# Tokens of an attention tile ordered column by column instead of row by row, in a hybrid convolution and neighbourhood-attention block on Trainium2

## The chip, the cores and the metric

The kernel runs on one core of one Trainium2 chip. The metric is the device time of one execution in microseconds (us); lower is better. A core has five engines that run their own instruction queues: TensorE (PE, matmuls and transposes), VectorE (DVE), ScalarE (ACT), GpSimd (POOL) and SyncE (SP, which here only issues DMAs). Sixteen DMA engines move data between the chip's memory (DRAM here) and the on-chip memory, whose 128 partitions are the rows of every tile. A line such as L411 is line 411 of the kernel before.

## The reference

One layer of a bidirectional encoder block on 1024 tokens of 1024 channels, in float32. The tokens form a grid of 16 rows by 64 columns (token = 64 * row + column).

```python
def reference(x, ...):
    h = rms_norm(x, norm1_g)
    a, gate, q, k, v = split(h @ w_in)              # 512 columns each
    conv_out = silu(layer_norm(dwconv31(a * sigmoid(gate)) + dw_bias))   # along the 1024 tokens
    q, k = rms_norm per head of 64 (8 heads)
    attn_out = neighbourhood_attention(q, k, v, rpb)
    x = x + concat([conv_out, attn_out]) @ w_out
    h = rms_norm(x, norm2_g)
    return x + (silu(h @ w_gate) * (h @ w_up)) @ w_down                  # 2816 hidden columns
```

In the attention, every query sees a window of 8 grid rows by 16 grid columns, clamped inside the grid, and a learned bias `rpb` by the offset of row and column is added to the scores before the softmax.

## The kernel before

**Tokens and tiles.** Up to the attention, a tile of 128 tokens is two whole grid rows (`t` of 0 to 7 in `nat`, `head_sq`, `head_T`). From the queries on, a tile is a rectangle of 8 grid rows by 16 grid columns: tile `4 * rh + cb` holds the rows `8 * rh` to `8 * rh + 7` and the columns `16 * cb` to `16 * cb + 15`. All 128 queries of such a tile share one window of 12 rows by 24 or 32 columns of keys (`WIN`). The order of the 128 tokens inside the rectangle is free, as long as every place agrees that lays tokens out or reads them. In the kernel before they stand row by row: position `16 * i + j` for row `i` and column `j`.

**Where the order appears.** Five places know it.

- `head_T` (L403 to L413) transposes the normalised queries of two grid rows on TensorE into a PSUM tile `zt` and copies them with two ScalarE activations (L411, one for each grid row) into `qT`, in the order of the rectangles.
- `table` (L592 to L603) loads the bias tables. `tf[rh, ty]` lies in DRAM as [8 rows, 16 columns, 8 heads, 12 * window columns]; a table in on-chip memory has one partition for each query of the rectangle, so the DMA (L601) reads 128 rows in the order of the queries. There are three kinds of column block (`ty`) and two row halves (`rh`).
- `conv_silu` (L777 to L783) transposes the normalised convolution output, which is in the natural order of tokens, applies SiLU on ScalarE, and splits the result into a rounded part `hi` (ScalarE, L107) and a remainder `lo` (VectorE, L111). Both are written into `cm` in the order of the rectangles, so that each tile of the output projection reads 128 adjacent columns.
- `rows` (L785 to L787) gives the DRAM view of the 128 tokens of a rectangle. `load_x2` (L789) uses it to load the residual `x`, and
- `store` (L1221) uses it for the output, half of the channels at a time.

Everything between these places (scores, softmax, output projection, second norm, feed-forward block) works on tiles of 128 tokens and needs no order.

**Order of the work.** The program is scheduled by hand. `nat` and `glu_step` run the input projections as three matmuls for each block (`mac`, L113 to L117, since each operand is held as `hi` and `lo`), with small jobs (`woven`, taken by `weave`) between the blocks; the queries' transposes are such a job, seven blocks into the next projection. Before them, ScalarE takes the squares of the next tile (`head_sq`), VectorE scales it (`head_scale`, `zn`). The depthwise convolution runs beside this on VectorE, with a few taps on ScalarE and GpSimd.

The attention goes over eight rectangles in the order `order` (L617), four steps `i` each, with two heads to a step: `score_mm` (L629), `score_max` (L641, which adds the table), `score_exp` (L646), `score_norm` (L657, GpSimd), `flip` (L665, transposes), `weigh` (L681). SyncE issues the loads it needs in program order: the tables of the first three rectangles, and windows of the values `vw` from DRAM (`load_vw`, L613, whose source is [4 rows, 24 or 32 columns, 512]); then the table `tab[1, 3]`, the table `tab[0, 1]` in step 4, a window in step 6, `tab[1, 1]` in step 8 and a window in step 12.

After the attention, the output projection `pj` of the left half of the channels takes the attention's rows first; the eight `conv_silu` calls are woven between its blocks, one after every second token tile, and its last blocks read `cm`. `resid` adds `x2`. The feed-forward block uses Strassen's seven products in both of its matmuls; `finish` adds up a quarter of the output and calls `store`, on SyncE's queue for three quarters and on ScalarE's queue for the last one (`m4`), four stores of [128 tokens, 512 channels] each.

Of the kernel before, what the change touches and what calls it, by code (L numbers as in the profile page):

```python
# [8 lines left out]
AF = mybir.ActivationFunctionType  # L9
# [15 lines left out]
GW = 64  # L25
# [42 lines left out]
def build(ctx, tc, a):  # L68
    nc = tc.nc
    pe, act, dve, pool = nc.tensor, nc.scalar, nc.vector, nc.gpsimd  # L70
# [5 lines left out]
    def T(tag, shape, bufs, name, dt=F32):  # L76
        return sb.tile(shape, dt, tag=tag, bufs=bufs, name=name)

    def G(name, dt=F32):
        return T("G", [P, 1024], 22, name, dt)  # L80
# [4 lines left out]
    def H(name, dt=F32):  # L85
        return T("H", [P, 4096], 6, name, dt)
# [13 lines left out]
    def tp(name):  # L100
        return ps.tile([P, 512], F32, tag="tp", bufs=2, name=name)
# [4 lines left out]
    def split(hi, lo, src, sub=(pool,)):  # L106
        act.copy(hi, src)  # L107
        n = src.shape[-1] // len(sub)
        for i, eng in enumerate(sub):
            sl = slice(i * n, (i + 1) * n)  # L110
            eng.tensor_tensor(*[w[..., sl] for w in (lo, src, hi.bitcast(F32))], OP.subtract)  # L111
# [140 lines left out]
    for _ in range(11):  # L252
# [3 lines left out]
    qgs = T("qgs", [P, 1], 1, "qgs")  # L256
    dve.tensor_scalar(qgs, qg, HD ** -0.5, None, op0=OP.mult)
    t1 = [dr.tile([NH, 16, 15, ncol], F32, name=f"t1{ty}") for ty, ncol in enumerate((24, 32, 24))]
    tf = {(rh, ty): dr.tile([8, 16, NH, AR * t1[ty].shape[-1]], F32, name=f"tf{rh}{ty}")
          for rh in range(2) for ty in range(3)}  # L260
# [118 lines left out]
    qT, kT = H("qT").rearrange("p (c s) -> p c s", s=S), H("kT").rearrange("p (c s) -> p c s", s=S)  # L379
# [23 lines left out]
    def head_T(n, t, zn):  # L403
        pt = tp(f"zt{n}{t}")
        for c in range(4):
            pe.transpose(pt[:, c * P:(c + 1) * P], zn[:, c * P:(c + 1) * P], ident)
        if n == 0:
            q5 = qT.rearrange("p c (h b i j) -> p c h b i j", h=2, b=4, j=16)
            p5 = pt.rearrange("p (c i b j) -> p c i b j", c=4, i=2, j=16)
            for i in range(2):  # L410
                act.activation(q5[:, :, t // 4, :, 2 * (t % 4) + i, :], p5[:, :, i], AF.Copy, scale=qgs)  # L411
        else:
            act.activation(kT[:, :, t * P:(t + 1) * P], pt.rearrange("p (c s) -> p c s", s=P), AF.Copy, scale=kg)  # L413

# [22 lines left out]
    def head_post(n, t, z, lag=7):  # L437
        def f(n_taps):
            sd = head_sq(n, t, z)
            pump(2 + {(1, 5): 3, (0, 1): 2}.get((n, t), 0))  # L440
            zn = head_scale(n, t, z, sd)
            pump(1)
            woven.extend([lambda: None] * lag)
            woven.append(lambda: head_T(n, t, zn))
        return f
# [145 lines left out]

    def table(rh, ty):  # L592
        n = AR * t1[ty].shape[-1]
        src = tf[rh, ty].rearrange("i j h c -> (i j) (h c)")
        if rh == 0 and ty == 0:
            parts = [(G(f"tab{k}")[:, :n * min(3, NH - 3 * k)], 3 * k) for k in range(3)]
        else:
            parts = [(H(f"tab{rh}{ty}")[:, :NH * n], 0)]
        heads = []
        for w, h0 in parts:  # L600
            nc.sync.dma_start(w, src[:, h0 * n:h0 * n + w.shape[-1]])  # L601
            heads += [w[:, o:o + n] for o in range(0, w.shape[-1], n)]
        return heads  # L603

# [100 lines left out]
    for t in range(6):  # L705
        value(t)
        if t == 2:
            while aside_dma:
                behind()
            tab[0, 0] = table(0, 0)  # L710
        if t == 3:
            tab[1, 0] = table(1, 0)
            tab[0, 3] = table(0, 2)
# [18 lines left out]
    cm, x2, xn = [], {}, {}  # L732
# [44 lines left out]
    def conv_silu(h, c):  # L777
        y = tp(f"z{h}{c}")
        for i in range(4):
            pe.transpose(y[:, i * P:(i + 1) * P], xh[4 * h + i][:, c * P:(c + 1) * P], ident)  # L780
        act.activation(y, y, AF.Silu, bias=lnb[:, c:c + 1], scale=lng[:, c:c + 1])
        hi, lo = [w[:, c, h * 512:(h + 1) * 512].rearrange("p (b i j) -> p i b j", b=4, j=16) for w in cm]
        split(hi, lo, y.rearrange("p (i b j) -> p i b j", b=4, j=16), (dve,))  # L783

    def rows(ap, t):  # L785
        rh, cb = divmod(t, 4)
        return ap.rearrange("(h i w) d -> h i w d", h=2, w=GW)[rh, :, cb * 16:cb * 16 + 16, :]  # L787

    def load_x2(t):  # L789
        x2[t] = G(f"x2{t}")  # L790
        nc.sync.dma_start(x2[t], rows(a["x"], t))
# [84 lines left out]
    proj(4, 0, acc0[4], range(4, 8))  # L876
    act.activation(warm, eps, AF.Silu)
    conv_silu(0, 0)
    proj(5, 0, acc0[5], range(4, 8))
    for t in range(6):  # L880
        load_x2(t)
    later = [(0, c) for c in range(1, 4)] + [(1, c) for c in range(4)]
    woven.extend(lambda q=q: conv_silu(*q) for q in later)
    for ts in (range(4), (4, 5)):
        for k in range(4):
# [335 lines left out]
    def store(p, t, w):  # L1221
        tok, d = {"m2": (0, 0), "m3": (0, 1), "m4": (1, 0), "m7": (1, 1)}[p]
        (nc.scalar if p == "m4" else nc.sync).dma_start(
            rows(a["out"], 4 * tok + t)[:, :, d * 512:(d + 1) * 512], w)
# [34 lines left out]
    for s, p in enumerate(SEQ):  # L1259
        for k in range(QF - 2):  # L1260
            n = s * QF + k
# [34 lines left out]
```

## Time and profile before

| | |
|---|---|
| time, median of 3 runs | 1057.92 us (1056.41 to 1058.7) |
| the profiled execution | 1058.55 us |
| its span, first to last instruction | 1056.8 us |
| mean granted TensorE clock | 0.997 |
| TensorE busy | 1044.2 us (99%) |
| VectorE, ScalarE, GpSimd busy | 696.0 (66%), 452.0 (43%), 382.2 (36%) us |
| moved by DMA | 144.06 MB, mean 136 GB/s |

How to read it: TensorE's busy share counts a matmul that is in the array, also a slow one. The chain that ended last is followed back from the last instruction; in it the words "DMA tab<-tf" stand for the time from the issue of a table load to its landing. In a table of stretches each row gives the stretch, its length, the busy time and number of instructions of TensorE, its weight loads, VectorE, ScalarE and GpSimd, then the granted clock, the busy share of the 16 DMA engines and what they moved in GB/s. In a list in order of time, each row gives the start, the duration, the engine with the line, and in brackets the idle time before it with what ended it.

### The profile page before, as it was taken

Reading aid. Unit: us, or ns where it says so; the run is one execution under the profiler, and the core shown is the slowest. Engines: PE = TensorE matmul, PEld = TensorE weight load, DVE = VectorE, ACT = ScalarE, POOL = GpSimd, SP = SyncE. Lnnn points to the kernel's source line nnn. Section 1 sums busy time; section 2 is a strip of 40 time slices with the busy share of each in tenths; the row PEclk is TensorE's granted clock in tenths of the full one; section 3 lists DMA queues with packets and bytes.
Section 4 is the critical chain, followed back from the end, with each engine's and each line's share of the span. In section 5 each row is a group of like instructions: output and inputs, shape, how many; then the busy total and the mean of one; then the engine's idle time right before and its main releaser. Section 6 shows DMA issues by size and latency. Waiting matters only on the chain.

```text
span 1056.8 us, 14098 instructions
## 1 busy us (share of the span) xinstructions
PE 1044.2 (99%) x5090; PEld 852.8 (81%) x5090; DVE 696.0 (66%) x1048; ACT 452.0 (43%) x987; POOL 382.2 (36%) x301
## 2 busy tenths in 40 slices
PE   9999999999999999999999999999999999999997
PEld 8788888877677887788888888888888888888886
DVE  5788997877665257665564564655656567758883
ACT  6556347737776244532223323232232444433441
POOL 1036765514551302444544445544455200002310
PEclk9999999999999999999999999999999999999999
DMA  9326781245505422133322333232232597634641
GB/s 353 147 62 212 221 256 44 75 152 164 165 26 165 134 100 80 41 109 109 110 100 90 110 113 109 79 130 100 82 133 73 191 327 270 209 100 129 208 130 41
DMA packets 68405, 144.06 MB, mean 136 GB/s; under 512 B 12528, under 2 KB 21232, under 8 KB 67696
## 3 DMA queue, kind: packets, MB, share of 16 engines
q1 hardware_dynamic: 66352, 139.68, 39.4%
q10 hardware_dynamic: 1984, 3.48, 1.0%
q8 instruction: 40, 0.66, 0.3%
q14 instruction: 29, 0.24, 0.1%
HBM read 103.99 MB, written 44.76 MB: 141 GB/s over the span
## 4 chain that ended last, share of the span: by engine, by line
PE 90%; DMA 4%; DVE 2%; ACT 2%; issue 1%; POOL 0%; SPq 0%; ACTq 0%; DVEq 0%; POOLq 0%
PE B L115 6%; PE B L117 6%; PE B L116 6%; PE A L115 4%; PE D L115 4%; PE D L117 4%; PE A L117 4%; PE D L116 4%; PE A L116 4%; PE z L115 3%; PE z L117 3%; PE z L116 3%; DMA tab<-tf 3%; PE gl L115 3%; PE gl L117 3%; PE gl L116 3%
## 5 line engine op out<-in xcount | busy, mean ns | idle before, releaser
L336 DVE SCALAR_TENSOR_TENSOR cv<-u,par,cv 128x1009 f32<-128x1009 f32 (+14 forms) x92 | 117.5, 1277 | 2.3
L362 POOL TENSOR_TENSOR pa<-pa,pr 128x1022 f32<-128x1022 f32 (+5 forms) x24 | 58.0, 2416 | 48.4 <-ACT pr L361 48.0
L107 ACT CAST op<-sr 128x512 fp32r<-128x512 f32 x77 | 47.7, 619 | 51.8 <-PE B2d L117 23.2
L111 DVE TENSOR_TENSOR op<-sr,op 128x512 fp32r<-128x512 f32 x77 | 57.8, 751 | 16.2 <-ACT op L107 16.2
L1079 DVE TENSOR_TENSOR g<-B,g 128x512 f32<-128x512 f32 x22 | 15.2, 691 | 79.1 <-PE B L117 79.1
L1251 POOL TENSOR_TENSOR ou<-ou,resm 128x512 f32<-128x512 f32 x8 | 12.1, 1523 | 144.0 <-DMA resm<-xd 142.2
L1088 ACT ACTIVATE D<-D 128x512 f32<-128x512 f32 x22 | 12.8, 582 | 113.2 <-DVE D L1087 113.2
L1074 DVE TENSOR_TENSOR u<-B,g 128x512 f32<-128x512 f32 x22 | 15.2, 691 | 62.1 <-PE B L117 62.1
L107 ACT CAST op<-wd 128x512 fp32r<-128x512 f32 x66 | 40.9, 619 | 32.1 <-DVE wd L1166 18.2
L935 DVE TENSOR_TENSOR ts<-gu,ts 128x512 f32<-128x512 f32 x44 | 51.0, 1159 | 0.8
L111 DVE TENSOR_TENSOR op<-wd,op 128x512 fp32r<-128x512 f32 x66 | 49.4, 748 | 2.2 <-ACT op L107 0.7
L657 POOL TENSOR_SCALAR e<-e,rs 128x288 f32<-128x288 f32 (+1 forms) x64 | 34.3, 548 | 43.4 <-DVE rs L655 35.5
L1077 ACT ACTIVATE A<-A 128x512 f32<-128x512 f32 x20 | 11.6, 582 | 76.3 <-PE A L117 76.3
L646 ACT ACTIVATE e<-e,mx 128x288 f32<-128x288 f32 (+1 forms) x64 | 36.5, 572 | 17.3 <-DVE mx L641 16.7
L641 DVE CUSTOM_DVE_ANT_0 e<-s,tab 128x288 f32<-128x288 f32 (+1 forms) x64 | 30.7, 499 | 17.8 <-PE s L629 11.2
L935 DVE TENSOR_TENSOR ts<-gu 128x512 f32<-128x512 f32 x22 | 34.0, 1547 | 0.0
L665 PEld LDWEIGHTS p<-ident,e 128*96 128x96 f32 (+1 forms) x192 | 20.4, 136 | 14.4 <-issue 8.7
L665 PE MATMUL p<-ident,e 128*96 128x128 f32 (+1 forms) x192 | 28.9, 286 | 3.1 <-POOL e L657 3.1
L389 ACT ACTIVATE sq<-z,r 128x64 f32<-128x64 f32 x96 | 28.6, 334 | 4.7 <-PE z L117 4.7
L361 ACT ACTIVATE pr<-u,par 128x1022 f32<-128x1022 f32 (+5 forms) x24 | 27.0, 1137 | 1.6 <-ACT vs L419 1.6
L986 POOL TENSOR_TENSOR xn<-xn,xn 128x512 f32<-128x512 f32 x4 | 6.9, 1725 | 57.0 <-DVE sn L986 53.6
L115 PE MATMUL B2d<-op 128*128 128x512 f32 x66 | 25.8, 391 | 0.0
(1040 smaller groups left out, 3469.3 us busy)
## 6 DMA issues: line engine op xcount, KB each, us to landing
gu<-in_gu SPq DMA_DIRECT2D x44, 512.0 KB
sr<-sd SPq DMA_DIRECT2D x77, 256.0 KB
sd<-sd SPq DMA_DIRECT2D x22, 512.0 KB
wd<-in_wd SPq DMA_DIRECT2D x44, 256.0 KB
sd<-g SPq DMA_DIRECT2D x33, 256.0 KB
x<-in_x SPq DMA_DIRECT2D x16, 512.0 KB
xd<-x SPq DMA_DIRECT2D x8, 512.0 KB
resm<-xd SPq DMA_DIRECT2D x16, 256.0 KB
```

Source lines behind the costliest of these rows:

```text
L107: act.copy(hi, src)
L111: eng.tensor_tensor(*[w[..., sl] for w in (lo, src, hi.bitcast(F32))], OP.subtract)
L115: pe.matmul(acc, lh, rh, start=start, stop=False, skip_group_check=True)
L116: pe.matmul(acc, lh, rl, start=False, stop=False, skip_group_check=True)
L117: pe.matmul(acc, ll, rh, start=False, stop=stop, skip_group_check=True)
L336: dve.scalar_tensor_tensor(acc[:, o], uc[:, i], dwk[:, c, t:t + 1], acc[:, o], OP.mult, OP.add)
L362: pool.tensor_tensor(pa[:, o], pa[:, o], pr[:, o], OP.add)
L641: dve.tensor_tensor_reduce(out=es[i][:, hh], in0=s[hh], in1=tab[rh, cb][2 * hp + hh], scale=-1.0, scalar=3.0e38, op0=OP.add, op1=OP.min, a ...
L646: act.activation(e, e, AF.Exp, bias=mx.pop((i, hh)), scale=-1.0, accum_out=sums[i][:, hh:hh + 1])
L657: pool.tensor_scalar(es[i][:, hh], es[i][:, hh], rs[:, hh:hh + 1], 1.0, op0=OP.mult, op1=OP.mult)
L665: pe.transpose(pt[:m, g * P:(g + 1) * P], es[i][:, hh, g * m:(g + 1) * m], ident)
L935: dve.tensor_tensor(o, l, r, OP.subtract)
```

## The change

The tokens of a rectangle stand column by column: position `8 * j + i` for row `i` and column `j`. The five places change together.

```diff
-            q5 = qT.rearrange("p c (h b i j) -> p c h b i j", h=2, b=4, j=16)
+            q5 = qT.rearrange("p c (h b j i) -> p c h b j i", h=2, b=4, j=16)
             p5 = pt.rearrange("p (c i b j) -> p c i b j", c=4, i=2, j=16)
             for i in range(2):
-                act.activation(q5[:, :, t // 4, :, 2 * (t % 4) + i, :], p5[:, :, i], AF.Copy, scale=qgs)
+                act.activation(q5[:, :, t // 4, :, :, 2 * (t % 4) + i], p5[:, :, i], AF.Copy, scale=qgs)
...
     def table(rh, ty):
         n = AR * t1[ty].shape[-1]
-        src = tf[rh, ty].rearrange("i j h c -> (i j) (h c)")
+        src = tf[rh, ty].rearrange("i j h c -> j i (h c)")
...
-            nc.sync.dma_start(w, src[:, h0 * n:h0 * n + w.shape[-1]])
+            nc.sync.dma_start(w, src[:, :, h0 * n:h0 * n + w.shape[-1]])
...
         act.activation(y, y, AF.Silu, bias=lnb[:, c:c + 1], scale=lng[:, c:c + 1])
-        hi, lo = [w[:, c, h * 512:(h + 1) * 512].rearrange("p (b i j) -> p i b j", b=4, j=16) for w in cm]
+        hi, lo = [w[:, c, h * 512:(h + 1) * 512].rearrange("p (b j i) -> p i b j", b=4, j=16) for w in cm]
         split(hi, lo, y.rearrange("p (i b j) -> p i b j", b=4, j=16), (dve,))
 
     def rows(ap, t):
         rh, cb = divmod(t, 4)
-        return ap.rearrange("(h i w) d -> h i w d", h=2, w=GW)[rh, :, cb * 16:cb * 16 + 16, :]
+        return ap.rearrange("(h i w) d -> h w i d", h=2, w=GW)[rh, cb * 16:cb * 16 + 16, :, :]
```

In `head_T` and `conv_silu` the writes that went in runs of 16 adjacent words now go to words that are 8 apart; in the second, VectorE also reads `hi` that way. In `table` the source becomes [16 columns, 8 rows, row of the table] instead of [128, row of the table]. In `rows`, and so in `load_x2` and `store`, the DRAM side becomes [16 columns, 8 rows, channels] instead of [8 rows, 16 columns, channels]. The number of bytes, of matmuls and of instructions stays as it was, and nothing is issued in another place.

## The prediction

> **What bounds the kernel now.** I read the head of the page first, then the chain that ended last in order of time, then the table of stretches, the tiles that the change touches, and the last stores. The profiled execution took 1058.55 us, 1.8 us more than its span; it stands 0.6 us above the median of the runs, 1057.92. I work out shifts of the span and add them to the median.
>
> ```profile
> span 1056.8 us, 14098 instructions
> PE 1044.2 (99%) x5090; PEld 852.8 (81%) x5090; DVE 696.0 (66%) x1048; ACT 452.0 (43%) x987; POOL 382.2 (36%) x301
> 242.75 15.79 DMA tab<-tf
> 261.57 16.97 DMA tab<-tf
> ```
>
> TensorE is busy through nearly the whole span, and the change alters no matmul in shape or number. It can therefore count only where TensorE waits, or after its last matmul. Three such places touch edited lines: the two bias-table loads in the chain, the SiLU of the convolution, and the last store.
>
> **The last store.** Next come two issues on ScalarE's queue in order of time, and the table of stretches at the end.
>
> ```profile
> 1047.18 1.21 ACTq L1223 DMA_DIRECT2D out_dram<-ou  x1
> 1051.26 0.61 ACTq L1223 DMA_DIRECT2D out_dram<-ou  x1
> core 0: us, PE busy (x) PEld busy (x) DVE busy (x) ACT busy (x) POOL busy (x), PEclk, DMA share, GB/s
> 1047.18:1048.40 1.22, 1.22 (x7) 1.03 (x6) 0.58 (x1) 0.00 (x0) 0.00 (x0) 1.00 0.00 0
> 1048.50:1049.60 1.10, 1.10 (x6) 0.92 (x5) 0.43 (x2) 0.00 (x0) 0.00 (x0) 1.00 0.51 58
> 1051.60:1052.60 1.00, 0.00 (x0) 0.00 (x0) 0.00 (x0) 0.00 (x0) 0.00 (x0) 1.00 0.52 174
> 1054.60:1055.50 0.90, 0.00 (x0) 0.00 (x0) 0.00 (x0) 0.00 (x0) 0.00 (x0) 0.50 0.46 173
> 1055.50:1056.70 1.20, 0.00 (x0) 0.00 (x0) 0.00 (x0) 0.00 (x0) 0.00 (x0) 0.50 0.00 0
> ```
>
> Four stores of 256 KB (262 kB) close the kernel, and the DMA engines stay at a share of 0.52: eight of sixteen. That is the outer count of the pattern `rows` hands over (8 grid rows of 16 tokens). At 174 GB/s a store needs 1.5 us, but the accumulators come 1.4 us apart (the first and the fourth issue, 4.08 over three), so a backlog forms: the last one, issued at 1051.26 and ready to move about 1.25 us later (as the first was), ends only at 1055.5. Afterwards the outer count is 16 columns. On sixteen engines at twice the rate a store takes 0.75 us, the queue is empty when the last comes, and it ends at 1053.3: 2.2 us earlier. If it starts as slowly as the first did (58 GB/s over 1.1 us, doubled to 116, so 128 kB of the 262, then 0.4 us), it ends at 1054.0, 1.5 us earlier. I take **-1.9 us**, nearer to the warm end, since the store before it is then only some 0.6 us past. [...]
>
> **The convolution's SiLU.** Each of eight `conv_silu` calls writes `hi` on ScalarE and `lo` on VectorE, in runs of 16 adjacent words now and with a step of 8 words after; VectorE also reads `hi` with that step. First the two operations, then the chain around their first use, ScalarE and VectorE there, and two forms of a VectorE operation of the same size.
>
> ```profile
> L107 ACT CAST cm<-z x8: 587/587/588, 331.4 to 346.3; 128x512 fp32r<-128x512 f32 x8
> L111 DVE TENSOR_TENSOR cm<-z,cm x8: 691/692/693, 332.0 to 347.0; 128x512 fp32r<-128x512 f32 x8
> 331.80 0.23 PE pj L117
> 332.03 0.50 PE pj L115
> ...
> 332.77 0.49 PE pj L117
> ...
> 333.94 0.44 PE z L780 x4
> ...
> 336.67 0.39 PE pj L117
> 334.41 0.75 ACT L781 ACTIVATE z<-z,par 128x512 f32<-128x512 f32 x1 [2.43 <-PE z L780]
> 336.24 0.75 ACT L781 ACTIVATE z<-z,par 128x512 f32<-128x512 f32 x1 [0.46 <-PE z L780]
> 335.81 0.69 DVE L111 TENSOR_TENSOR cm<-z,cm 128x512 fp32r<-128x512 f32 x1 [3.11 <-ACT cm L107]
> L935 DVE TENSOR_TENSOR ts<-gu,ts 128x512 f32<-128x512 f32 x44 | 51.0, 1159 | 0.8
> L935 DVE TENSOR_TENSOR ts<-gu 128x512 f32<-128x512 f32 x22 | 34.0, 1547 | 0.0
> ```
>
> A matmul here takes 0.23 us, so 0.50, 0.49 and 0.39 are waits for the first tile's `hi`, its `lo`, and the second tile's `lo`. They already bind: whatever `hi` and `lo` grow by is added at the first tile, and once more at the second, whose transposes stand behind the delayed matmuls. The third tile has slack: its SiLU starts at 336.24 and would be through in 0.75 + 0.99 + 1.16 = 2.9 us, while from 337.06 nine matmuls of 0.23 and two sets of transposes of 0.44 still come before its first use, to 340.0. No row has a single-word step, so I bound its price from both sides. Below: nothing; a gain is excluded, as no word less is moved. Above: the slowest VectorE operation of this size, 1547 against 692, a factor of 2.24; in between stands the other form at 1159, a factor of 1.68. I take 1.68: it is the nearest row with two streams from the same memory delayed. That is 587 to 986 ns on ScalarE (+0.40) and 692 to 1159 on VectorE (+0.47), 0.87 together, twice: **+1.7 us** on the path. Later tiles come every 1.83 us and ScalarE needs 0.75 + 0.99 of that, so nothing more is late; two buffers give a tile 3.67 us, and 0.44 + 0.75 + 0.99 + 1.16 fit.
>
> [...]
>
> **The queries.** `head_T` has two ScalarE writes per tile, which change in the same way.
>
> ```profile
> L411 ACT ACTIVATE qT<-zt,qgs x16: 467/472/477, 160.3 to 202.1; 128x256 f32<-128x256 f32 x16
> 170.10 0.75 DVE L399 SCALAR_TENSOR_TENSOR zn<-z,r,r 128x512 f32<-128x512 f32 x1
> 171.52 0.60 PE L406 MATMUL zt<-ident,zn 128*128 128x128 f32 x4
> ```
>
> The pair stands ahead of the next tile's squares on ScalarE; these give `zn`, which ends at 170.85, and the transposes that read it start at 171.52. That 0.67 us is the cover, in each of seven periods. At 1.68 the pair costs 2 x 0.32 = 0.64 us: hidden, barely. At 2.24 it costs 1.17 and 0.50 shows each time, 3.5 us. The score matmuls read `qT` in plain slices as before.
>
> **The tables and the residual loads.** Here are sizes, VectorE's waits, the issue of a table, and stretches around both table loads and the residual loads.
>
> ```profile
> tab<-tf SPq DMA_DIRECT2D x2, 1536.0 KB
> tab<-tf SPq DMA_DIRECT2D x1, 1152.0 KB
> 258.70 0.46 DVE L641 CUSTOM_DVE_ANT_0 e<-s,tab 128x288 f32<-128x288 f32 x1 [1.92 <-DMA tab<-tf]
> 278.70 0.56 DVE L641 CUSTOM_DVE_ANT_0 e<-s,tab 128x384 f32<-128x384 f32 x1 [3.73 <-DMA tab<-tf]
> L601 SPq DMA_DIRECT2D tab<-tf x8: 319/383/2386, 187.9 to 261.6; - x8
> 217.00:220.00 3.00, 3.00 (x15) 2.46 (x14) 2.93 (x3) 1.48 (x2) 0.47 (x1) 1.00 1.03 421
> 248.00:253.00 5.00, 5.00 (x51) 3.86 (x52) 3.78 (x14) 3.81 (x12) 2.34 (x5) 1.00 1.04 273
> 254.50:261.50 7.00, 6.56 (x76) 4.92 (x73) 4.29 (x18) 4.97 (x17) 2.94 (x7) 1.00 0.26 106
> 278.70:283.00 4.30, 2.32 (x12) 1.45 (x14) 3.78 (x14) 3.47 (x11) 2.30 (x4) 0.93 0.58 179
> 283.00:288.00 5.00, 5.00 (x42) 3.40 (x40) 3.11 (x12) 3.12 (x10) 2.79 (x5) 0.72 0.57 171
> 322.00:331.00 9.00, 8.88 (x48) 7.09 (x47) 6.65 (x18) 5.20 (x10) 2.01 (x3) 1.00 0.47 133
> 335.00:343.00 8.00, 8.00 (x44) 6.43 (x43) 2.77 (x4) 5.84 (x10) 0.00 (x0) 1.00 0.51 204
> ```
>
> A table arrives last on four engines (share 0.26): the window loads `vw`, whose outer count is 4, keep those busy. The table's rows stay whole, 128 of them on 16 engines, so a quarter still ends there, and I cost the new order at **nothing**. Its issue in two dimensions may take 0.61 us as the stores' does, not 0.38; the backlog on the four engines hides the 0.23, and costs 0.23 per table if it is gone. Should the reading order cost or save, the second wait takes it in full. The residual loads go to sixteen engines too; their readers stand behind the matmuls of that stage, which cover the loads already, so nothing is won.
>
> Sum: -1.9 + 1.7 + 0 + 0 = -0.2, so **1057.7 us**. What a measurement of this kernel can tell from no change is about 0.2%, or 2.1 us.
>
> **Rivals.** *Strides are free*: only the tail is left, -1.5 to -2.2, 1056.0 at -1.9. For it: no row shows a penalty for any order of words. *Strides are dear* (slower): at 2.24 the first two tiles cost 2 x (0.73 + 0.86) = 3.2, the queries 3.5, less 1.9: +4.8, 1062.7. It decides once a query write exceeds 0.81 us, where the cover of 0.67 is used up. *Tables read slower*: rows that an engine reads now lie 16 grid positions apart. The residual loads moved 133 GB/s at a share of 0.47 early and 204 at 0.51 later, 1.41 times apart per engine, which shows that loads can run at the lower rate. The four engines carry a quarter of three tables, 1.08 MB, about 10.2 us at 106 GB/s; 41% more is 4.2, so 1061.9. *Tables come sooner*: at 248 the traffic runs at 273 GB/s where 421 was reached at 217. If the order relieves this, the second wait goes: 1.98 us idle in 278.7 to 283, and 0.3 and 1.4 for clocks of 0.93 and 0.72, together 3.7, 1054.0; POOL's normalisation is late next. *Stores stay on eight engines*: no tail, +1.7, 1059.6.
>
> **How the numbers follow.** Forecast 0.40; free strides 0.14, half of it beyond 0.2% since its range ends at -2.2; dear strides 0.19; slower tables 0.12; sooner tables 0.12; stores on eight 0.03. Faster: 0.07 + 0.12 = 0.19. Slower: 0.31. Same: 0.50. The range, 1055.0 to 1062.5, holds the forecast, free strides, slower tables and stores on eight, and cuts into the outer two.
>
> **What would show it.** The last stretch: a DMA share near 1 instead of 0.52 and an end near 1053.5 on this scale. `hi` near 0.99 and `lo` near 1.16 us; the waits around 332 and 337 longer by 0.87 each. The query writes near 0.79, the transposes without a wait. VectorE's waits for `tab` still 1.9 and 3.7. I am wrong if a strided write costs over twice the plain one, or if either table wait moves by over 1 us.

## The result and the profile after

The changed kernel takes **1063.33 us** (median of 5 runs, 1063.19 to 1064.72) where the kernel before takes 1057.92 (also 5 runs by then, 1056.41 to 1058.7): a ratio of 1.0056, 95% interval 1.0042 to 1.007, so some 5.4 us slower. The forecast was 1057.7, with a range that ended at 1062.5, and "same" as the likeliest outcome. It was wrong: the time lies above the range. The profiled execution took 1064.72 us, 6.2 more than that of before.

First the head of the page after, and the chain of waits from 225 to 300 us (start, duration, what).

```profile
span 1063.0 us, 14098 instructions
PE 1047.6 (99%) x5090; PEld 854.2 (80%) x5090; DVE 699.0 (66%) x1048; ACT 458.0 (43%) x987; POOL 381.9 (36%) x301
...
242.60 19.36 DMA tab<-tf
265.00 19.19 DMA tab<-tf
```

The instructions are as many as before. Each of the two table loads takes longer from its issue: 19.36 us instead of 15.79, and 19.19 instead of 16.97. Their readers on VectorE, in order of time, and the last issue on ScalarE's queue:

```profile
262.13 0.46 DVE L641 CUSTOM_DVE_ANT_0 e<-s,tab 128x288 f32<-128x288 f32 x1 [5.49 <-DMA tab<-tf]
284.35 0.56 DVE L641 CUSTOM_DVE_ANT_0 e<-s,tab 128x384 f32<-128x384 f32 x1 [3.47 <-DMA tab<-tf]
1059.21 0.55 ACTq L1223 DMA_DIRECT2D out_dram<-ou  x1
```

These three rows stood at 258.70, 278.70 and 1051.26 before. The differences split the loss: +3.43 at the first reader, **+5.65** at the second, **+7.95** at the last store's issue, and +6.2 at the end of the span (1063.0 against 1056.8). So the tables cost 5.65 us in this execution, what lies between them and the last store 2.3, and the tail gives back 1.75.

How the 5.65 come about can be read from the chain. The first of the two loads takes 3.57 us longer and is issued 0.15 earlier, so its reader starts 3.43 later. The second load is issued 2.87 us after that reader in both kernels (261.57 after 258.70, 265.00 after 262.13), so it starts 3.43 later too, and it takes 2.22 us longer itself: together 5.65. VectorE's two waits show this only in part: the first grew by 3.57 us (5.49 against 1.92), the second shrank by 0.26 (3.47 against 3.73), since VectorE, too, comes to it later. Now the table of stretches:

```profile
core 0: us, PE busy (x) PEld busy (x) DVE busy (x) ACT busy (x) POOL busy (x), PEclk, DMA share, GB/s
217.00:220.00 3.00, 3.00 (x15) 2.49 (x14) 2.93 (x3) 1.62 (x2) 0.32 (x1) 1.00 0.99 262
248.00:253.00 5.00, 5.00 (x52) 3.76 (x52) 3.63 (x14) 3.94 (x12) 2.18 (x5) 1.00 1.07 204
254.50:261.50 7.00, 5.30 (x64) 4.04 (x60) 1.34 (x5) 2.72 (x9) 1.59 (x4) 1.00 0.55 131
258.70:262.00 3.30, 1.10 (x21) 0.85 (x16) 0.00 (x0) 0.00 (x0) 0.00 (x0) 1.00 0.25 101
265.00:268.00 3.00, 3.00 (x13) 1.70 (x12) 1.65 (x8) 1.63 (x5) 0.85 (x3) 0.50 0.26 100
1058.00:1059.00 1.00, 0.45 (x2) 0.03 (x1) 0.51 (x1) 0.00 (x0) 0.00 (x0) 1.00 0.71 205
1059.00:1060.00 1.00, 0.00 (x0) 0.00 (x0) 0.18 (x1) 0.00 (x0) 0.00 (x0) 1.00 0.85 211
1060.00:1061.00 1.00, 0.00 (x0) 0.00 (x0) 0.00 (x0) 0.00 (x0) 0.00 (x0) 1.00 0.69 158
1061.00:1061.90 0.90, 0.00 (x0) 0.00 (x0) 0.00 (x0) 0.00 (x0) 0.00 (x0) 0.76 0.51 173
1061.90:1063.00 1.10, 0.00 (x0) 0.00 (x0) 0.00 (x0) 0.00 (x0) 0.00 (x0) 0.50 0.00 0
```

Four things are to be seen. Where tables are loaded, the DMA engines are as busy as before (shares of 0.99 and 1.07, before 1.03 and 1.04) and move less: 262 GB/s instead of 421 at 217, 204 instead of 273 at 248. This phase of all sixteen engines is what lasts longer: from 254.5 to 261.5 the share is 0.55 where before it was 0.26, four engines alone; once those four are alone here too, from 258.7 on, they move 101 GB/s, hardly less than the 106 of before. After the longer first stall the clock stands at 0.50 from 265 to 268, and TensorE, busy through all of the stretch, gets through 13 matmuls. On the path this cost nothing that the trace shows: the second reader starts at 284.35, 0.16 us after the second load lands (265.00 + 19.19 = 284.19), and VectorE still waits 3.47 us for it. And the last store ends at 1061.9, 2.7 us after its issue; before it was 4.2 (1051.26 to 1055.5).

Then the tiles that the change writes: `qT` and `cm`.

```profile
L411 ACT ACTIVATE qT<-zt,qgs x16: 731/783/789, 160.2 to 202.2; 128x256 f32<-128x256 f32 x16
L107 ACT CAST cm<-z x8: 1102/1138/1172, 336.9 to 354.3; 128x512 fp32r<-128x512 f32 x8
L111 DVE TENSOR_TENSOR cm<-z,cm x8: 1145/1175/1219, 338.1 to 355.6; 128x512 fp32r<-128x512 f32 x8
```

The query writes went from 472 to 783 ns (forecast: about 0.79 us), the remainder `lo` from 692 to 1175 (forecast 1159), the rounded part `hi` from 587 to 1138 (forecast 986).

### The profile page after: what moved, and what is told of

Same layout as the page of the kernel before. It is cut to its first block, busy times and chain, and to the rows that moved or that the text cites. A ratio compares the mean times of both kernels' runs of the same rounds, so it can differ in the third digit from the quotient of the medians.

```text
span 1063.0 us, 14098 instructions
## 1 busy us (share of the span) xinstructions
PE 1047.6 (99%) x5090; PEld 854.2 (80%) x5090; DVE 699.0 (66%) x1048; ACT 458.0 (43%) x987; POOL 381.9 (36%) x301
## 4 chain that ended last, share of the span: by engine, by line
PE 88%; DMA 6%; DVE 2%; ACT 2%; issue 1%; SPq 0%; POOL 0%; DVEq 0%; POOLq 0%; ACTq 0%
PE B L117 6%; PE B L115 6%; PE B L116 6%; PE A L115 4%; PE D L117 4%; PE A L117 4%; PE D L115 4%; PE D L116 4%; PE A L116 4%; DMA tab<-tf 4%; PE z L115 3%; PE z L117 3%; PE z L116 3%; PE gl L115 3%; PE gl L116 3%; PE gl L117 3%
## 5 line engine op out<-in xcount | busy, mean ns | idle before, releaser
L361 ACT ACTIVATE pr<-u,par 128x1022 f32<-128x1022 f32 (+5 forms) x24 | 27.0, 1138 | 1.6 <-ACT vs L419 1.6
```

## The experiments

### One part at a time

Four kernels make one part of the change each, beginning from the kernel before; then the whole change ran beside two of them. With one part alone the tokens stand in two orders at once, so these four do not compute the reference's output; they are there for their time. `e3_rows_only` has the two lines in `rows`:

```diff
-        return ap.rearrange("(h i w) d -> h i w d", h=2, w=GW)[rh, :, cb * 16:cb * 16 + 16, :]
+        return ap.rearrange("(h i w) d -> h w i d", h=2, w=GW)[rh, cb * 16:cb * 16 + 16, :, :]
```

> The kernel before with the new order in rows alone (residual loads and stores), so its output has the tokens of a rectangle in another order. Theory: only the tail gains; from the last matmul to the end 4.5 us instead of 6.3, and the time falls by 1.8 to about 1056.1 us. Rival: residual loads on sixteen engines crowd out the weight loads beside them, and part of the 1.8 is lost before the last matmul: 1057 or more.

`e4_cm_only` has the line in `conv_silu`:

```diff
-        hi, lo = [w[...].rearrange("p (b i j) -> p i b j", b=4, j=16) for w in cm]
+        hi, lo = [w[...].rearrange("p (b j i) -> p i b j", b=4, j=16) for w in cm]
```

> The kernel before with the stepped writes in conv_silu alone, so the output projection reads its convolution half in another token order than its attention half. Theory: hi takes 1.14 us and lo 1.17 us as in the changed kernel, the matmuls behind the first tiles wait, and the time rises by 2.3 us to 1060.2. Rival: the dearer writes cost only 1.1 us each in the changed kernel because of other traffic at that moment, and the time rises by under 1 us.

`e9_queries_only` has the two lines in `head_T`:

```diff
-            q5 = qT.rearrange("p c (h b i j) -> p c h b i j", h=2, b=4, j=16)
+            q5 = qT.rearrange("p c (h b j i) -> p c h b j i", h=2, b=4, j=16)
...
-                act.activation(q5[:, :, t // 4, :, 2 * (t % 4) + i, :], p5[:, :, i], AF.Copy, scale=qgs)
+                act.activation(q5[:, :, t // 4, :, :, 2 * (t % 4) + i], p5[:, :, i], AF.Copy, scale=qgs)
```

> The kernel before with the changed writes of the queries alone (so the queries stand in another order than the bias). If the writes at 0.78 us are hidden, as the trace of the changed kernel says: within 1 us of the kernel before, first score matmul at the same time within 0.5 us. The version with whole tables (first experiment) was 1.5 us over the sum of stores and SiLU; if the queries are what it paid: +1.5 us.

`e8_tables_only` has the two lines in `table`:

```diff
-        src = tf[rh, ty].rearrange("i j h c -> (i j) (h c)")
+        src = tf[rh, ty].rearrange("i j h c -> j i (h c)")
...
-            nc.sync.dma_start(w, src[:, h0 * n:h0 * n + w.shape[-1]])
+            nc.sync.dma_start(w, src[:, :, h0 * n:h0 * n + w.shape[-1]])
```

> The kernel before with the changed source of the table loads alone (so the bias rows stand in another order than the queries). Theory A (the load in groups of eight rows is what costs, by itself): the changed kernel was 5.4 us over the one before, stores alone gave -2.3 and the convolution's SiLU alone +1.9, so 5.8 are left for the tables and the queries; +4 to +6 us, 1062 to 1064 where the kernel before takes 1058, both table waits longer than before, traffic in the quiet stretch after 189.4 at about 280 GB/s instead of 410. Theory B (the tables are late only together with the slower query and SiLU writes or the residual loads on sixteen engines): under +2 us.

And `e10_change` is the changed kernel once more.

> The changed kernel once more beside its parts. If the parts add up: the time of the kernel before plus the four differences measured alone (stores -2.3, SiLU +1.9, tables and queries as in this call) within 1 us, so 1062 to 1064. If the parts interact (a table that comes later covers a slow write, or the other way), the sum misses by over 1.5 us.

Medians against the kernel before, run beside each:

| part | this, us | before, us | difference | ratio, 95% interval |
|---|---|---|---|---|
| rows (loads of `x`, stores) | 1055.94 | 1058.23 | -2.29 | 0.9979, 0.997 to 0.9989 |
| conv SiLU | 1060.13 | 1058.23 | +1.90 | 1.0024, 1.0013 to 1.0034 |
| queries | 1057.77 | 1058.29 | -0.52 | 0.9999, 0.9989 to 1.0008 |
| tables | 1064.13 | 1058.29 | **+5.84** | 1.0053, 1.0036 to 1.007 |
| sum of the four | | | +4.93 | |
| the whole change | 1063.22 | 1058.29 | +4.93 | 1.0052, 1.0037 to 1.0067 |

The parts add up as far as can be told. That the sum meets the whole to the second digit is luck: each difference has an interval of 1 to 2 us to either side, some 3 us for the sum against the whole, so a smaller interaction of the parts is not excluded. The queries cost nothing that can be seen although each write takes 0.3 us longer. The tables alone make the kernel slower by as much as the whole change, and the rival reading, that they are late only together with the slower writes or the wider residual loads, falls. The chain and the quiet stretch of `e8_tables_only`, in which the first table loads and little else moves:

```profile
242.73 19.00 DMA tab<-tf
264.76 19.75 DMA tab<-tf
...
189.40:190.40 1.00, 1.00 (x9) 0.86 (x7) 0.96 (x2) 0.60 (x3) 0.78 (x1) 1.00 0.68 211
190.40:191.40 1.00, 1.00 (x6) 0.82 (x5) 0.96 (x2) 1.00 (x7) 1.00 (x1) 1.00 1.16 289
191.40:192.40 1.00, 1.00 (x6) 0.83 (x5) 1.00 (x1) 1.00 (x9) 0.63 (x1) 1.00 0.94 235
```

The same stretch of the kernel before:

```profile
189.40:190.40 1.00, 1.00 (x8) 0.88 (x7) 0.96 (x2) 0.60 (x3) 0.75 (x1) 1.00 0.80 308
190.40:191.40 1.00, 1.00 (x6) 0.81 (x5) 0.96 (x2) 1.00 (x6) 1.00 (x1) 1.00 1.05 410
191.40:192.40 1.00, 1.00 (x6) 0.83 (x5) 1.00 (x1) 1.00 (x9) 0.65 (x1) 1.00 0.96 346
```

Per engine that is 410 / (16 x 1.05) = 24 GB/s before and 289 / (16 x 1.16) = 16 after, with no other work in the way. A row of a table costs its engine half as much time again. What remains is why.

### Why a table row takes longer

In the source [16 columns, 8 rows, row of the table] two things differ from [128, row]. The rows that follow each other in a load lie 16 grid positions apart in DRAM; and the transfer is laid out in 16 groups of eight, so that an engine may get other partitions to write (which it gets, no trace shows). `e1_tables_whole` removes both: it starts from the changed kernel, stores `tf` column by column, and loads 128 adjacent rows.

```diff
-    tf = {(rh, ty): dr.tile([8, 16, NH, AR * t1[ty].shape[-1]], F32, ...)
+    tf = {(rh, ty): dr.tile([16, 8, NH, AR * t1[ty].shape[-1]], F32, ...)
...
-            nc.sync.dma_start(tf[rh, ty][i, :, :, a0 * ncol:(a0 + 8) * ncol],
+            nc.sync.dma_start(tf[rh, ty][:, i, :, a0 * ncol:(a0 + 8) * ncol],
...
-        src = tf[rh, ty].rearrange("i j h c -> j i (h c)")
+        src = tf[rh, ty].rearrange("j i h c -> (j i) (h c)")
```

> The changed kernel, with the bias tables kept in DRAM in the new order as well, so that a table load is again 128 adjacent rows in one dimension. Theory A (the table loads are the main loss): the two waits of VectorE for a table go back from 9.0 us to about 5.6, the attention loses its 5.6 us of delay, and the time falls from 1063.3 to about 1057.7 us. Rival B (the attention is late because the query writes grew to 0.78 us on ScalarE): the waits for tables stay near 9 us and the time stays near 1063.

Measured: 1059.35 against 1058.23, ratio 1.0014 (1.0004 to 1.0024). Most of the loss is gone, and VectorE waits 4.3 us for a table, once. But it is 2.0 us above the sum of the other three parts (-2.29 + 1.90 - 0.52 = -0.9, against +1.1), so the time alone does not show that all of the 5.84 came back (each of these medians has an interval of some 1 us to either side, so that 2.0 is at the edge of what they can tell). In its trace all of it did: the second load's reader starts at 278.36, where it stood at 278.70 before and at 284.35 in the changed kernel.

```profile
260.77 17.42 DMA tab<-tf
...
278.36 0.28 DVE e L641
```

That execution took 1057.27 us, the shortest of the eleven. The fill of `tf` also writes in another pattern here; `e5_pairs` below has the same fill and is faster than the kernel before, so a cost of 2 us of the fill is not likely. Where the 2.0 lie stays open.

`e2_tables_gap` keeps the adjacent rows and brings the groups back: 64 unused words after every eight rows of a table, so that the load can only go out as 16 times 8 rows.

```diff
-    tf = {(rh, ty): dr.tile([16, 8, NH, ...], F32, ...)
+    tfp = {(rh, ty): dr.tile([16, 8 * NH * AR * ncol + 64], F32, ...)
+    tf = {k: w[:, :-64].rearrange("j (i h c) -> j i h c", i=8, h=NH) for k, w in tfp.items()}
...
-        src = tf[rh, ty].rearrange("j i h c -> (j i) (h c)")
+        src = tf[rh, ty].rearrange("j i h c -> j i (h c)")
```

> The kernel of the run before, with 256 unused bytes in DRAM after every eight rows of a table. The rows are read in the same adjacent order, but the load can no longer be written in one dimension and goes out as 16 groups of 8 rows, as in the changed kernel. Theory S (the way the rows are dealt to DMA engines and partitions is what is slow): back to about 1063 us, a DMA rate near 200 to 230 GB/s from 244 to 253 us and waits for tables near 9 us. Rival D (the order in which DRAM rows are read is what is slow): as the run before, about 1057.7 us, 270 GB/s or more and waits near 5.6 us.

Measured: 1068.9 against 1058.23, ratio 1.0103 (1.0085 to 1.012). Its chain in the attention, and its waits from 60 to 230 us (engine and tile, what it waited for: sum, times, longest):

```profile
247.06 18.76 DMA tab<-tf
268.85 19.30 DMA tab<-tf
...
ACT w01h L107 <- DMA w01r<-in_qkv: 11.8, 1, 11.8
ACT w02h L107 <- DMA w02r<-in_qkv: 6.5, 1, 6.5
```

The table loads take 18.76 and 19.30 us, as in the changed kernel, although the rows are adjacent, and the packets of the first table (3456 bytes, one table row of three heads) have a median of 234 ns, beside 232 in the changed kernel and 135 before: **the distance of the rows in DRAM is not the cause, the groups are.** The kernel is slower still because everything in the attention comes 4.5 us later (247.06 against 242.60): the padded tables are filled with other writes, and ScalarE waits 11.8 and 6.5 us for weights in that part of the program. That is a side effect of the experiment, on which nothing here rests.

Then two cuts by partitions. Their reading supposes that in a load of groups each engine carries one group, and so writes eight neighbouring partitions. The DMA shares fit that (0.51 to 0.54 with eight groups in `e6_halves`, 0.25 to 0.27 with four in `e7_middle`); which engine writes which partition no trace shows. Both kernels cut the first column block's tables of the first row half into pieces by partitions; the source, the issue in groups and the rows stay as in the changed kernel. `e6_halves` cuts at 0-63 and 64-127; `e7_middle` sends 32-95 first, then 0-31, then 96-127.

```diff
-            nc.sync.dma_start(w, src[:, :, h0 * n:h0 * n + w.shape[-1]])
+            for lo, hi in (CUT if rh == ty == 0 else ((0, 16),)):
+                nc.sync.dma_start(w[lo * 8:hi * 8], src[lo:hi, :, h0 * n:h0 * n + w.shape[-1]])
# e6_halves: CUT = ((0, 8), (8, 16));  e7_middle: CUT = ((4, 12), (0, 4), (12, 16))
```

> The changed kernel with the first table's three loads cut in two, partitions 0 to 63 and 64 to 127, eight groups of 8 rows each, in the quiet stretch after 188 us. Theory W (engines that write partitions 32 apart stand in each other's way: a load that deals eight neighbours to each engine makes engines 0 and 4, 1 and 5 and so on meet): eight engines at the low rate, 14 to 16 GB/s each, as the changed kernel's sixteen. Rival V (a load in groups of 8 rows is slow by itself, wherever it goes): the same. This run is the partner of the next.

> As the run before, with the same loads cut as partitions 32 to 95 (eight groups), 0 to 31 and 96 to 127 (four groups each). Every engine still gets eight neighbouring partitions, but in no load are two engines 32 partitions apart inside the same half of 64. Theory W: about 25 GB/s for each busy engine in the stretch after 188 us, as in the kernel before. Rival V: 14 to 16 GB/s each, as with the halves.

Stretches of the first table of `e6_halves`:

```profile
192.00:193.00 1.00, 1.00 (x6) 0.81 (x5) 1.00 (x1) 1.00 (x8) 0.69 (x1) 1.00 0.51 142
193.00:194.00 1.00, 1.00 (x6) 0.83 (x5) 0.05 (x1) 0.97 (x8) 0.00 (x0) 1.00 0.54 138
194.00:195.00 1.00, 1.00 (x6) 0.84 (x5) 0.80 (x2) 1.00 (x2) 0.00 (x0) 1.00 0.53 135
```

And of `e7_middle`:

```profile
191.00:192.00 1.00, 1.00 (x7) 0.79 (x6) 0.96 (x2) 1.00 (x8) 1.00 (x1) 1.00 0.48 121
192.00:193.00 1.00, 1.00 (x6) 0.84 (x5) 0.46 (x1) 1.00 (x8) 0.09 (x1) 1.00 0.44 159
193.00:194.00 1.00, 1.00 (x6) 0.84 (x5) 0.39 (x2) 0.97 (x4) 0.00 (x0) 1.00 0.27 100
194.00:195.00 1.00, 1.00 (x6) 0.76 (x5) 1.00 (x2) 0.51 (x1) 0.41 (x1) 1.00 0.25 100
```

With 0-63 at a time, eight engines move 138 / (16 x 0.54) = 16 GB/s each from 193 to 194: as slow as in the changed kernel, though only half of the engines work. In the middle cut they move 159 / (16 x 0.44) = 23 GB/s from 192 to 193, and later 25 with four engines at work: as in the kernel before. Single stretches scatter: the one before that shows only 121 / (16 x 0.48) = 16, and in `e6_halves` 193 GB/s at a share of 0.52 from 190.4 to 191.4 make 23. So the packets are the better measure. Those of 3456 bytes, from 185 to 225 us, have a median of 135 ns before, 232 in the changed kernel, 205 in `e6_halves`, and 135 in `e7_middle`. So neither the groups nor the number of engines at work is slow as such; what differs between the two cuts is **which partitions are written at the same time**. With one group to an engine, both have pairs of engines that write partitions 32 apart: 0-7 and 32-39 when 0-63 is loaded, 32-39 and 64-71 when 32-95 is; the slow pairs lie in one half of 64, the others across the middle. That the engines of a slow pair stand in each other's way is the author's reading of these two runs; what they would share no trace shows.

Neither cut could help the whole time: the first table is not the one that is late, and the two in the chain were left in groups. Each ran once (1065.33 and 1064.98, where the changed kernel's runs lie between 1062.87 and 1064.82), and one run can't tell such a difference from none.

### Writes in pairs of words

`e5_pairs` starts from `e1_tables_whole`. The transposes of the queries and of the convolution multiply by a permuted identity, which puts tokens of both grid rows side by side, so that `qT` and `cm` are written two adjacent words at a time instead of one.

```diff
-            pe.transpose(pt[:, c * P:(c + 1) * P], zn[:, c * P:(c + 1) * P], ident)
+            pe.transpose(pt[:, c * P:(c + 1) * P], zn[:, c * P:(c + 1) * P], ident if n else identp)
...
-            for i in range(2):
-                act.activation(q5[:, :, t // 4, :, :, 2 * (t % 4) + i], p5[:, :, i], AF.Copy, scale=qgs)
+            act.activation(q5[:, :, t // 4, :, :, 2 * (t % 4):2 * (t % 4) + 2], p5, AF.Copy, scale=qgs)
...
-        hi, lo = [w[...].rearrange("p (b j i) -> p i b j", b=4, j=16) for w in cm]
+        hi, lo = [w[...].rearrange("p (b j i k) -> p i b j k", b=4, j=16, k=2) for w in cm]
```

> The first run's kernel (new order everywhere, tables whole), with the transposes of the queries and of conv_silu made against a permuted identity, so that the two grid rows of a tile come out as neighbours; qT and cm are then written in runs of two adjacent words, 8 words apart, and the two query writes become one of 512 elements. Theory P (a step over single words is what costs; a run of two words is as good as a plain one): hi back to 0.59 us and lo to 0.69 us, the 2.5 us of waits in the convolution's SiLU gone, only the tail's 1.8 us left, about 1056.4 us. Rival Q (every hop of 8 words costs, whatever the run): hi and lo at about half of their growth, 0.86 and 0.93, and the time near 1057.7. A third possibility, that hops cost the same for any run under 16, would leave hi and lo at 1.14 and 1.19 and the time at 1059.

Measured: 1056.56 against 1058.13, ratio 0.9985 (0.9976 to 0.9994). Of the versions that keep the whole computation it is the fastest, and it beats the kernel before by 1.6 us. Its two writes of `cm`:

```profile
L107 ACT CAST cm<-z x8: 637/665/694, 331.0 to 346.1; 128x512 fp32r<-128x512 f32 x8
L111 DVE TENSOR_TENSOR cm<-z,cm x8: 700/709/714, 331.7 to 346.8; 128x512 fp32r<-128x512 f32 x8
```

With two words VectorE is at the old price (709 against 692 ns) and ScalarE close to it (665 against 587); with one, both were at 1.1 us and over. So the price here was for a step at every single word: of the 551 ns that it cost ScalarE 473 went with pairs, and of VectorE's 483, 466.

## Why the prediction was wrong

**The tables: this step failed.** "The table's rows stay whole, 128 of them on 16 engines, so a quarter still ends there, and I cost the new order at nothing." The rows do stay whole and sixteen engines do carry them, but the step counted engines and bytes and left out which partitions are written at the same time. Measured: 16 instead of 24 GB/s per engine, 3.57 and 2.22 us more from issue to landing, 5.65 us at the second reader, 5.84 alone. The term should have had two ends, from 0 to the rival's +4.2, in the range and not only in a chance of 0.12. The place was named in part: "the second wait takes it in full" did not hold. The first wait took 3.57 us, and the second did not grow; the second reader is late because its load was issued after the late first reader and was slow itself. What the prediction took for the stores, how many engines a shape gets, it also took to be enough for the tables.

**"Tables read slower" had the right outcome by the wrong mechanism.** It blamed rows that lie 16 grid positions apart; adjacent rows in groups were as slow (18.76 and 19.30 us). It was also too small, and in the wrong place: it put 41% more time on the four engines' backlog, +4.2. Those four, once alone, kept their rate (101 GB/s against 106); the phase of all sixteen slowed, in both loads of the chain.

**The convolution's SiLU: mechanism right, size short.** The waits on the critical path, as forecast, are for the first and second tiles; here is the chain of the changed kernel there:

```profile
336.93 1.11 ACT cm L107
338.07 1.17 DVE cm L111
339.28 0.50 PE pj L117
...
341.73 1.14 ACT cm L107
342.89 1.16 DVE cm L111
344.09 0.50 PE pj L117
...
346.54 1.16 ACT cm L107
347.72 1.22 DVE cm L111
348.99 0.66 PE z L780 x4
```

`hi` and `lo` grew by 0.55 and 0.48 us, 1.03 together instead of 0.87, so twice gives 2.1 instead of 1.7. The third tile had its slack, as forecast. But the chain goes on through the fourth (its `hi` at 346.54, its `lo` at 347.72): the transposes two tiles on, which need its place in one of the two buffers, wait for its `lo` and take 0.66 us instead of 0.44. Two tiles later this comes once more (0.66 at 352.87). "Two buffers give a tile 3.67 us, and 0.44 + 0.75 + 0.99 + 1.16 fit" failed here by a little: the fourth tile takes 3.66 us from the start of its transposes (345.28) to the end of its `lo` (348.94), and with the hand-over 3.71. Twice 1.03 and twice 0.22 make 2.5, beside 2.3 in the rows above between the second table and the last store. Alone it measured +1.90. The mis-sized number is the factor: 1.68, taken from a VectorE row, held on VectorE (1.70) and not on ScalarE (1.94 for 512 elements, 1.66 for the queries' 256). That this row is long because two streams come from one memory, as the choice supposed, no run shows.

**The queries: right.** 783 ns against about 790, and no time lost: two writes cost 0.62 us more per tile, under the cover of 0.67. "Strides are dear" needed a write over 0.81 us; it came within 0.03 of that point.

**The tail: right in size, half right in the reason.** -1.75 in the trace, -2.29 measured alone, forecast -1.9 with -1.5 to -2.2. The backlog is gone as forecast: the last store takes 2.7 us from its issue to its end, not 4.2. But that an outer count of 16 puts a store on sixteen engines at twice the rate was the author's estimate, from a share of 0.52 at an outer count of 8, and no run shows it: what the changed kernel shows is 205, 211 and 158 GB/s at shares of 0.71, 0.85 and 0.69, so more than eight engines, but not about 350 near 1. Per engine that is 18, 16 and 14 GB/s where the stores before had 174 / (16 x 0.52) = 21. Why was not tried.

**In sum:** -1.75 for -1.9, +2.3 for +1.7, 0 for 0, and +5.65 for 0. Without the last term the forecast would have been 0.8 us off in this execution; the two smaller errors, +0.15 and +0.6, do not cancel each other.

## What to carry to other kernels

A transfer has an address pattern on two sides: before a DMA is reshaped, ask not only how many engines it gets, but which partitions they will write at the same time (here the first table's packets took 205 ns where eight groups went to partitions 0-63, and 135 where the load was cut into 32-95, 0-31 and 96-127). Where an edit's cost is unseen in the trace and the wait behind it is already binding, no term of "nothing" is safe: put its upper bound in the range. Where an order must be stepped in on-chip memory, moving the permutation into a transpose so that two adjacent words are written together removed most of the price here (1138 to 665 ns on ScalarE, 1175 to 709 on VectorE, beside 587 and 692 for runs of 16).

## What the runs showed of the hardware

- A load to 128 partitions in 16 groups of 8 ran on sixteen engines at 16 GB/s each (`e8_tables_only`, share 1.16), and the same bytes as 128 plain rows at 24 (the kernel before, share 1.05). Eight engines loading 0-63 in groups of eight moved 16 GB/s each from 193 to 194 in `e6_halves` (packets of 3456 bytes: median 205 ns), and in `e7_middle`, which loads 32-95 first, 23 from 192 to 193 (135 ns).
- ScalarE writing 512 floats with a step of 8 words took 1138 ns instead of 587; 256 floats took 783 instead of 472. VectorE, which also read one source with that step, took 1175 instead of 692. In pairs of words (`e5_pairs`) it was 665 and 709.
- A DMA share near 1 went with different rates: 1.07 with 204 GB/s stood where 1.04 with 273 stood before, and 0.99 with 262 where 1.03 with 421 stood.
- VectorE's wait of 5.49 us for a table was followed by a granted clock of 0.50 from 265 to 268, and the second reader still started 0.16 us after its load's landing; in the kernel before, a wait of 1.92 us was followed at the same place by a clock of 1.00:

```profile
261.00:264.00 3.00, 3.00 (x31) 2.15 (x31) 2.71 (x13) 2.49 (x9) 1.64 (x4) 1.00 0.25 95
```
